# Ten weight tiles of a decoder kernel, each 96 bytes longer

## The chip, the cores and the metric

The kernel runs on one core of a Trainium2 chip. The metric is the device time of one execution in microseconds (us). Before the change the median of two runs is 1173.27 us, from 1173.14 to 1173.4.

A core has a matrix engine (TensorE, PE in the profile, with PEld for its weight loads), three engines for elementwise work (VectorE or DVE, ScalarE or ACT, GpSimd or POOL) and a sync engine (SP) that issues transfers. They work on SBUF, an on-chip memory of 128 partitions. A tile of [128, 1024] float32 takes 4096 bytes in each partition, at the same address in all of them; "address" below means this address within a partition. PSUM is the small memory that the matrix engine writes.

## What is computed

A decoder of two layers over 512 tokens of width 1024, in float32. Layer 0 mixes tokens by stick-breaking attention, layer 1 by a diagonal state-space model with a gated output. After each mixer comes a gated feed-forward block of width 2816 with a short causal convolution. All norms are scaled and shifted by vectors that one matrix-vector product makes from a conditioning vector `c`. Cut to what matters:

```
for i in range(2):
    mod = silu(c) @ w_mod[i] + b_mod[i]           # six vectors of 1024
    h = rms_norm(x) * (1 + sc1) + sh1
    y = attention(h) if i == 0 else ssm(h)         # weights w_qkv, w_o / w_in, w_glu, w_o
    x = x + g1 * y
    h = rms_norm(x) * (1 + sc2) + sh2
    up = conv3(h @ w_up[i]) + conv_b[i]            # 1024 -> 2 * 2816
    x = x + g2 * ((silu(gate(up)) * val(up)) @ w_down[i])
out = rms_norm(x) * (1 + sc) + sh
```

## The kernel before

**Products in three parts.** All large products run in the matrix engine's float32r type. To keep the precision, each operand is split into a high part and a low part, and `mm3` (L169) issues three matmuls: high by high (L171), high by low (L174), low by high (L175). In the names of the profile `up_h` is the high part of a tile of `w_up`, `up_l` its low part, and `hH`, `hL` are those of the activations. Each matmul has the weights as its stationary operand (128 x 128, loaded by a LDWEIGHTS just ahead of it) and 512 or 256 columns of activations as the moving one. In the projection to `v` alone (L592, L652) it is the other way round: the activations are loaded and the weights move.

**How a weight tile is made.** `load_w` (L147) takes a tile `raw` of [128, 1024] float32 from the pool `wp` (tag `wraw`, three buffers) and has SP load 512 KB into it (L163). ScalarE copies it into the high part `wh` (L165), and VectorE subtracts that from `raw` into the low part `wl` (L166). High parts have the tag `wH`, low parts `wL`, with `NW = 5` buffers each (L161, L162): these are the ten tiles of the change. For `w_v` the same tags are used by `high` (L570) and for `wv0` (L605). A buffer is given out again when its last matmul has read it. `load_w(own=...)` (L158) takes other tiles instead: two weights at the head of a block have a pool of their own (`head_w`, L178), whose names in the profile are `upo`, `win` and `uph` with the number 0 or 1; their neighbours 2 and 3 use the ten tiles.

**Who orders the work.** The engines have a queue each and run in order. A planner puts the instructions in order by modelled times; `pe_pin` and `keep_in_program_order` fix some of them by hand, and `follow` (L141) ties the splits of the feed-forward blocks into one line on ScalarE and one on VectorE. Semaphores make every instruction wait for its operands, and for the last reader of the memory that it writes; pools with `reuse_waits="tile"` wait for just those earlier tiles whose addresses they take.

**Where tiles lie.** Pools stack up from the low end of SBUF in the order in which they are opened: `const`, `wp` (three `wraw`, five `wH`, five `wL`), `xp` (the residual `x`), `hp` (`hH`, `hL`), `np` (buffers of the norms), and above them the pools of the current block. The pools opened with `side="right"` stack down from the high end: `gemv` (`cact`, `wg`), and at times the pool of `head_w` or that of the last norm. Tiles are rounded up to 32 bytes. In the program's map of before, taken modulo 512 bytes:

| tiles | start modulo 512 |
|---|---|
| `wraw`, all ten of `wH` and `wL` | 320 |
| `x`, `hH`, `hL`, `acc`, `nt2`, most tiles of the blocks (`ca`, `gH`, `gL`, `kz`) | 320 |
| `sq`, `nt1`, `dg` | 64 |
| right side: `cact`, `wg`, high and low parts of `head_w` | 480 |

Where the two stacks come closest, in attention, 1184 bytes are free between them.

**Stages.** Attention takes the first 250 us of the profile, feed-forward block 0 the time to about 610 us, the state-space layer that to about 780 us, and feed-forward block 1 with the last norm the rest. In block 0 GpSimd prepares tables for the state-space layer (`ssm_prep`, L984), in steps placed between the block's units; its first write there is a memset of the tile `tb` (L1103), which takes memory that a `head_w` tile had held.

Of the kernel before, what the change touches and what calls it, by code (L numbers as in the profile page):

```python
# [9 lines left out]
F32R = mybir.dt.float32r  # L10
# [7 lines left out]
P = 128  # L18
T = 512
D = 1024  # L20
# [9 lines left out]
NC = T // CH  # L30
EPS = 1e-6
NW = 5
MIDK = 1
STATK = 0
HEADK = 6
# [54 lines left out]
def _trunk(ctx, tc, I, out, tap):  # L90
# [3 lines left out]
    def pool(name, bufs=1, **kw):  # L94
        return ctx.enter_context(tc.tile_pool(name=name, bufs=bufs, **kw))

    cp = pool("const")
    wp = pool("wp")
# [48 lines left out]
    def load_w(src, n=D, name="w", own=None, lined=False):  # L147
        raw = wp.tile([P, D], F32, tag="wraw", bufs=3, name=name + "_r")
        if isinstance(own, list):

            pin["load"] = SP.dma_start(raw, src)
            cols = slice(0, D // 2), slice(D // 2, D)
            for q, cs in enumerate(cols):
                pe_pin(S.activation(own[q], raw[:, cs], AF.Copy))
            for q, cs in enumerate(cols):
                pe_pin(V.tensor_tensor(own[2 + q], raw[:, cs], own[q].bitcast(F32), ALU.subtract))
            return own[:2], own[2:]
        if own:  # L158
            wh, wl = (own.tile([P, D], F32R, tag=name + g, name=name + g) for g in ("_h", "_l"))
        else:  # L160
            wh = wp.tile([P, D], F32R, tag="wH", bufs=NW, name=name + "_h")  # L161
            wl = wp.tile([P, D], F32R, tag="wL", bufs=NW, name=name + "_l")  # L162
        pin["load"] = SP.dma_start(raw[:, :n], src)  # L163
        order = follow if lined else lambda eng, fn: fn()
        order("S", lambda: S.activation(wh[:, :n], raw[:, :n], AF.Copy))  # L165
        pin["split"] = order("V", lambda: V.tensor_tensor(wl[:, :n], raw[:, :n], wh[:, :n].bitcast(F32), ALU.subtract))  # L166
        return wh, wl
# [10 lines left out]
    def head_w(srcs, nm):  # L178
        hx = ExitStack()
        own = hx.enter_context(tc.tile_pool(name=f"hw{nm}", bufs=1, side="right", reuse_waits="tile"))  # L180
        return hx, [load_w(src, name=f"{nm}{q}", own=own if q < 2 else None) for q, src in enumerate(srcs)]
# [72 lines left out]
    def pe_pin(ins):  # L254
        tc.keep_in_program_order(ins)
# [34 lines left out]
    def rstd_bc(R, cr, pl, pinned=False):  # L290
        bc = bank(pl, "rbc")
        ins = PE.matmul(bc[:, cr], ones, R["dg"][:, cr], start=True, stop=True)
        if pinned:
            pe_pin(ins)
        R["bc"][cr.start] = bc
# [68 lines left out]
    def out_proj(wsrc, rhs, gcol, acc2, nm, tail=TAIL, perm=False, n=D, after=lambda: None, part=(), last=None, head=None, getw=None, step=lambda: None, early={}):  # L364
        nk = len(rhs)
        whole = KD - (tail if acc2 is not None else 0)

        lined = getw is not None
        getw = getw or (lambda mt: early[mt] if mt in early else load_w(wsrc(mt), n=n, name=f"{nm}{mt}"))

        def cols(ap, cr):
            return half_cols(ap, cr) if perm and cr != FULL else ap[:, cr]

        def run(ps, w, cr, mid={}, k0=0, pinned=False):
            for k in range(k0, nk):
                if k in mid:
                    mid[k]()
                mm3(cols(ps, cr), wk(w, k), (cols(rhs[k][0], cr), cols(rhs[k][1], cr)), k == 0, k == nk - 1, k in mid or pinned)
# [32 lines left out]
        for q, (mt, w, ps) in enumerate(ws):  # L411
# [3 lines left out]
            if q == 2:  # L415
                mid[MIDK if nk > 6 else MIDN] = lambda: rstd_bc(R, ca, aux, True)
            run(ps, w, cb, mid, pinned=True)
# [12 lines left out]
    def ffn(l, R, prep=None, last=None, hook=lambda: None):  # L430
# [4 lines left out]
        with ExitStack() as fc:  # L435
# [11 lines left out]
            def split_next(lined=True):  # L447
                if todo:
                    src, n, nm = todo.pop(0)
                    made.append(load_w(src, n=n, name=nm, lined=lined))  # L450
# [95 lines left out]
    def attention(acc):  # L546
        with ExitStack() as av_, ExitStack() as ac:
# [20 lines left out]
                return raw  # L568

            def high(k):  # L570
                w = [wp.tile([P, D], F32R, tag=f"w{g.upper()}", bufs=NW, name=f"wv{k}_{g}") for g in "hl"]
                pe_pin(S.activation(w[0], raws[k], AF.Copy))
                return w

# [27 lines left out]
            pe_pin(SP.dma_start(raw0, I["w_v"][0:P, :]))  # L602
            raws = {1: loads(1)}
            SP.dma_start(small[:, NMOD:], I["small"][:, NMOD:])
            wv0 = [wp.tile([P, D], F32R, tag=f"w{g.upper()}", bufs=NW, name=f"wv0_{g}") for g in "hl"]  # L605
            idle = pin["idle"]
            gv_mul(1, 0)
            idle(NIDLE[2])
# [75 lines left out]
            prod0(vo[4:], HI)  # L684
            prod0(vo[4:], LO)
            w = high(1)
            for k in range(1, KD):
                def mid():
                    nxt[0] = high(k + 1) if k < KD - 1 else None
                    pe_pin(V.tensor_tensor(w[1], raws[k], w[0].bitcast(F32), ALU.subtract))  # L690
                    if k < KD - 1:
                        gv(1, k + 1)

                nxt = [None]
                gv(0, k)
                norm_tile(h, k, rb, a, mod[:, 0:KD], FULL, True, None, mid)
                if k + 2 < KD:
                    raws[k + 2] = loads(k + 2)
                prods(k, w)
                w = nxt[0]  # L700
# [771 lines left out]
    for k in range(KD):  # L1472
# [4 lines left out]
        if k:  # L1477
            pe_pin(V.tensor_tensor(acc, acc, sq, ALU.add))
    R = attention(acc)
    for k in range(KD):  # L1480
        tap(f"x1_{k}", x[k])
# [161 lines left out]
```

## Time and profile before

| | |
|---|---|
| median of two runs | 1173.27 us (1173.14 to 1173.4) |
| the profiled execution's own time | 1172.41 us |
| its span, first to last instruction | 1170.6 us |
| PE (matmul) busy | 1156.1 us, 99% of the span |
| PEld (weight load) busy | 966.5 us, 83% |
| DVE busy | 855.1 us, 73% |
| ACT busy | 564.7 us, 48% |
| POOL busy | 274.0 us, 23% |
| granted clock of the matrix engine, mean | 0.995 |
| moved by DMA | 211.01 MB, mean 180 GB/s |

A busy matmul lasts from its start to its modelled end, and the next one starts before that end. So the busy share says that the matrix engine always had something in flight, and the distance from one start to the next says how fast it went; the two are read apart in what follows. The rows of the groups have, after the name of the operation, the tiles written and read, the shape and the count, then the busy time in us and the mean duration of one in ns, then the idle time of the engine just before, with what ended it.

### The profile page before, as it was taken

How to read it: one execution, taken by the hardware profiler on the slowest of the kernel's cores; microseconds unless marked ns; L12 is line 12 of the kernel's file. 1: busy time of each engine (PE TensorE's matmuls, PEld its weight loads, DVE VectorE, ACT ScalarE, POOL GpSimd, SP SyncE). 2: the span in 40 equal slices, each digit the busy share in tenths (PEclk: the TensorE clock that was granted, in tenths of full speed). 3: DMA queues.
4: the chain of work that ended last, by engine and by line, in shares of the span. 5: the costliest groups of instructions: out<-in, count | busy, mean ns of one | idle time of the engine just before them, and what ended most of it. 6: DMA issues, size and time to landing. Idle time of an engine off the chain costs nothing.

```text
span 1170.6 us, 16595 instructions
## 1 busy us (share of the span) xinstructions
PE 1156.1 (99%) x6242; PEld 966.5 (83%) x6242; DVE 855.1 (73%) x1311; ACT 564.7 (48%) x896; POOL 274.0 (23%) x278
## 2 busy tenths in 40 slices
PE   8999999999999999999999999999999999999997
PEld 7888787798788878888889888789888888888887
DVE  6969889675997657697767698887698278734655
ACT  6755667456452234413346587547443144422443
POOL 2001110000398799979700000000000000000013
PEclk8999999999999999999999999999999999999999
DMA  8874555322267758697756598671176356432322
GB/s 326 297 267 138 193 174 169 126 91 70 75 206 252 236 165 250 203 306 242 236 148 221 172 350 286 206 253 54 43 231 219 103 157 187 130 120 74 93 68 73
DMA packets 91618, 211.01 MB, mean 180 GB/s; under 512 B 19601, under 2 KB 37905, under 8 KB 91538
## 3 DMA queue, kind: packets, MB, share of 16 engines
q1 hardware_dynamic: 78562, 191.08, 50.6%
q0 software_dynamic: 4656, 16.78, 4.3%
q10 hardware_dynamic: 8320, 2.10, 0.8%
q8 instruction: 49, 0.80, 0.3%
q14 instruction: 31, 0.25, 0.1%
HBM read 188.68 MB, written 21.24 MB: 179 GB/s over the span
## 4 chain that ended last, share of the span: by engine, by line
PE 80%; POOL 8%; DMA 4%; DVE 4%; ACT 1%; issue 1%; SPq 0%; POOLq 0%; ACTq 0%; DVEq 0%
PE up L171 11%; PE up L174 11%; PE up L175 11%; PE dn L171 5%; PE dn L174 5%; PE dn L175 5%; PE o L831 2%; PE t L815 2%; PE wo L171 1%; PE u L174 1%; PE u L171 1%; PE wo L174 1%; PE wo L175 1%; PE u L175 1%; PE q L175 1%
## 5 line engine op out<-in xcount | busy, mean ns | idle before, releaser
L171 PE MATMUL up<-hH,up_h 128*128 128x512 f32 x640 | 249.6, 390 | 0.3 <-DVE ca L465 0.3
L175 PE MATMUL up<-hH,up_l 128*128 128x512 f32 x640 | 249.2, 389 | 0.3 <-DVE up_l L166 0.3
L174 PE MATMUL up<-hL,up_h 128*128 128x512 f32 x640 | 249.2, 389 | 0.0
L465 DVE SCALAR_TENSOR_TENSOR ca<-up,small,ca 128x511 f32<-128x511 f32 (+1 forms) x176 | 131.7, 748 | 120.9 <-ACT ca L463 117.6
L171 PE MATMUL dn<-gH,dn_h 128*128 128x512 f32 (+1 forms) x394 | 145.0, 369 | 0.0
L174 PE MATMUL dn<-gL,dn_h 128*128 128x512 f32 (+1 forms) x394 | 144.4, 367 | 0.0
L175 PE MATMUL dn<-gH,dn_l 128*128 128x512 f32 (+1 forms) x394 | 144.4, 366 | 0.0
L171 PEld LDWEIGHTS up<-hH,up_h 128*128 128x128 f32 x640 | 120.1, 188 | 26.3 <-issue 1.7
L175 PEld LDWEIGHTS up<-hH,up_l 128*128 128x128 f32 x640 | 120.2, 188 | 25.6 <-DVE up_l L166 0.8
L174 PEld LDWEIGHTS up<-hL,up_h 128*128 128x128 f32 x640 | 120.2, 188 | 24.5
L463 ACT ACTIVATE ca<-up,small 128x512 f32<-128x512 f32 x88 | 68.2, 775 | 149.3 <-PE up L175 149.3
L1515 POOL TENSOR_SCALAR xa<-x,Anorm_out 128x256 f32<-128x256 f32 x7 | 5.8, 828 | 569.1 <-DVE x L359 569.1
L202 DVE SCALAR_TENSOR_TENSOR wg<-wg,cact 128x1024 f32<-128x1024 f32 x96 | 120.7, 1276 | 13.2 <-DMA wg<-in_w_modT_dram 13.1
L165 ACT ACTIVATE up_h<-up_r 128x1024 fp32r<-128x1024 f32 x80 | 84.2, 1052 | 80.1 <-PE dn L174 58.2
L166 DVE TENSOR_TENSOR up_l<-up_r,up_h 128x1024 fp32r<-128x1024 f32 x80 | 113.3, 1417 | 9.9 <-ACT up_h L165 9.0
L359 DVE SCALAR_TENSOR_TENSOR x<-dn,mod,x 128x512 f32<-128x512 f32 (+1 forms) x55 | 37.4, 680 | 72.4 <-PE dn L175 72.4
L171 PEld LDWEIGHTS dn<-gH,dn_h 128*128 128x128 f32 x394 | 74.3, 189 | 12.8 <-issue 0.6
L174 PEld LDWEIGHTS dn<-gL,dn_h 128*128 128x128 f32 x394 | 74.3, 189 | 12.1
L175 PEld LDWEIGHTS dn<-gH,dn_l 128*128 128x128 f32 x394 | 74.3, 189 | 12.1
L165 ACT ACTIVATE dn_h<-dn_r 128x1024 fp32r<-128x1024 f32 (+1 forms) x48 | 46.6, 982 | 48.7 <-PE dn L174 40.3
L166 DVE TENSOR_TENSOR dn_l<-dn_r,dn_h 128x1024 fp32r<-128x1024 f32 (+1 forms) x48 | 60.5, 1261 | 1.6 <-ACT dn_h L165 1.3
L481 ACT ACTIVATE gH<-gm 128x512 fp32r<-128x512 f32 x44 | 27.1, 617 | 69.3 <-DVE gm L477 69.3
(349 smaller groups left out, 2317.1 us busy)
## 6 DMA issues: line engine op xcount, KB each, us to landing
up_r<-in_w_up_dram SPq DMA_DIRECT2D x80, 512.0 KB
wg<-in_w_modT_dram SPq DMA_DIRECT2D x71, 512.0 KB
dn_r<-in_w_down_dram SPq DMA_DIRECT2D x32, 512.0 KB
wg<-in_w_modT_dram POOLq DMA_DIRECT2D x25, 512.0 KB, 4.8
wgs<-in_w_modT_dram SPq DMA_DIRECT2D x16, 512.0 KB
dn_r<-in_w_down_dram SPq DMA_DIRECT2D x16, 384.0 KB
wv_r<-in_w_v_dram SPq DMA_DIRECT2D x8, 512.0 KB
wk_r<-in_w_qk_dram SPq DMA_DIRECT2D x8, 512.0 KB
```

The source lines that it names most:

```text
L165: order("S", lambda: S.activation(wh[:, :n], raw[:, :n], AF.Copy))
L166: pin["split"] = order("V", lambda: V.tensor_tensor(wl[:, :n], raw[:, :n], wh[:, :n].bitcast(F32), ALU.subtract))
L171: ins = PE.matmul(ps, ah, bh, start=start, stop=False)
L174: PE.matmul(ps, ah, bl, start=False, stop=False)
L175: PE.matmul(ps, al, bh, start=False, stop=stop)
L202: mul = lambda: V.scalar_tensor_tensor(w, w, 1.0, cact, ALU.mult, ALU.mult, accum_out=raw[:, col:col + 1])
L359: add = lambda: V.scalar_tensor_tensor(xs, pv, gate, xs, ALU.mult, ALU.add)
L463: follow("S", lambda: S.activation(ca, ps, AF.Identity, bias=small[:, cb:cb + 1], scale=tapw[2]))
L465: follow("V", lambda: V.scalar_tensor_tensor(ca[:, q:], ps[:, :T - q], tapw[2 - q], ca[:, q:], ALU.mult, ALU.add))
L481: follow("S", lambda: S.activation(gh, m, AF.Copy))
L815: pe_pin(PE.transpose(pt[:, c:c + P], wts[pr][h2][i][:, j * P:(j + 1) * P], ident))
L831: pe_pin(PE.matmul(po[pr][h2 * HD:(h2 + 1) * HD, j * P:], vn[:, j, hd:hd + HD], src, start=j == 0, stop=j == 3))
```

## The change

The five `wH` and five `wL` buffers are allocated with 1024 + 24 float32 columns, 4192 bytes, and only the first 1024 columns are used. This holds at all three places that allocate under these tags. No instruction is added or removed.

```
+WPAD = 24
...
-            wh = wp.tile([P, D], F32R, tag="wH", bufs=NW, name=name + "_h")
-            wl = wp.tile([P, D], F32R, tag="wL", bufs=NW, name=name + "_l")
+            wh = wp.tile([P, D + WPAD], F32R, tag="wH", bufs=NW, name=name + "_h")[:, :D]
+            wl = wp.tile([P, D + WPAD], F32R, tag="wL", bufs=NW, name=name + "_l")[:, :D]
...
-                w = [wp.tile([P, D], F32R, tag=f"w{g.upper()}", bufs=NW, name=f"wv{k}_{g}") for g in "hl"]
+                w = [wp.tile([P, D + WPAD], F32R, tag=f"w{g.upper()}", bufs=NW, name=f"wv{k}_{g}")[:, :D] for g in "hl"]
...
-            wv0 = [wp.tile([P, D], F32R, tag=f"w{g.upper()}", bufs=NW, name=f"wv0_{g}") for g in "hl"]
+            wv0 = [wp.tile([P, D + WPAD], F32R, tag=f"w{g.upper()}", bufs=NW, name=f"wv0_{g}")[:, :D] for g in "hl"]
```

4192 is a multiple of 32, and 96 more than eight times 512. So the ten buffers begin at 320, 416, 0, 96, 192 (high) and 288, 384, 480, 64, 160 (low) modulo 512. Every tile stacked above them moves up by 960 bytes: what began at 320 then begins at 256, what began at 64 begins at 0. The `wraw` buffers below and the right side stay where they are.

## The prediction

> **What bounds the kernel now.** I read the page first, for the engine that sets the time and for the waits beside it.
>
> ```profile
> span 1170.6 us, 16595 instructions
> PE 1156.1 (99%) x6242; PEld 966.5 (83%) x6242; DVE 855.1 (73%) x1311; ACT 564.7 (48%) x896; POOL 274.0 (23%) x278
> PE 80%; POOL 8%; DMA 4%; DVE 4%; ACT 1%; issue 1%; SPq 0%; POOLq 0%; ACTq 0%; DVEq 0%
> L171 PE MATMUL up<-hH,up_h 128*128 128x512 f32 x640 | 249.6, 390 | 0.3 <-DVE ca L465 0.3
> L175 PE MATMUL up<-hH,up_l 128*128 128x512 f32 x640 | 249.2, 389 | 0.3 <-DVE up_l L166 0.3
> L174 PE MATMUL up<-hL,up_h 128*128 128x512 f32 x640 | 249.2, 389 | 0.0
> L171 PE MATMUL dn<-gH,dn_h 128*128 128x512 f32 (+1 forms) x394 | 145.0, 369 | 0.0
> L166 DVE TENSOR_TENSOR up_l<-up_r,up_h 128x1024 fp32r<-128x1024 f32 x80 | 113.3, 1417 | 9.9 <-ACT up_h L165 9.0
> ```
>
> The matrix engine is busy for 1156.1 of 1170.6 us, and four fifths of the chain that ended last are its own. Its largest groups wait for nothing: over 1,920 matmuls of `up` it stood idle 0.6 us, and only 0.3 of that for a weight's low part. Making the ten tiles sooner is therefore worth next to nothing; the change can only tell if it alters how fast matmuls follow each other. For that I read the chain in order of time, in two short stretches of feed-forward block 1, where a piece is the distance to the next start: first 512 columns, then 512 and 256 at the block's end.
>
> ```profile
> 1049.78 0.23 PE dn L175
> 1050.01 0.23 PE dn L171
> 1050.46 0.23 PE dn L175
> 1050.69 0.23 PE dn L171
> ...
> 1142.94 0.23 PE dn L175
> 1143.40 0.12 PE dn L175
> 1143.52 0.12 PE dn L171
> 1143.64 0.12 PE dn L174
> ```
>
> From one L171 to the next are three matmuls: 1050.69 - 1050.01 = 0.68 us, 227 ns each for 512 columns. For 256 columns it is 120 ns. The difference of 107 ns over 256 columns is 0.418 ns a column, so 512 columns stream in 214 ns and 256 in 107, and either way 13 ns are left over that do not depend on the columns. These 13 ns a matmul are all that a better place for the weights could win on this engine.
>
> **The change part by part.** It removes and adds no instruction, no transfer and no wait that I can find; it changes addresses. There are four kinds of reader and writer to go through.
>
> *Weight loads and matmuls.* Some 4,600 of the 6,242 matmuls take their weights from the ten tiles: 1,920 of `up`, 1,182 of `dn` (three times 394), about 1,500 of the projections and the output products. All of them run today with weights and activations both at 320 modulo 512. The trace has one group of loads that mixes two places: the heads of the feed-forward blocks, where `upo` 0 and 1 lie at 480, which is 32 modulo 64 as half of the new places are, and `upo` 2 and 3 in the ten tiles at 320. And it has loads from 64 (`q_sq`, `q_nt`) against a moving tile at 320. These are the views of the tiles, with the shortest, middle and longest duration in ns:
>
> ```profile
> L171 PEld LDWEIGHTS up<-hH,up_h x640: 186/188/192, 269.1 to 1125.8; 128*128 128x128 f32 x160
> L171 PEld LDWEIGHTS up<-hH,upo_h x56: 187/188/193, 259.2 to 286.9; 128*128 128x128 f32 x56
> L174 PEld LDWEIGHTS up<-hL,upo_h x56: 186/188/193, 259.6 to 287.1; 128*128 128x128 f32 x56
> L798 PEld LDWEIGHTS z<-kz,q_sq x32: 187/189/192, 82.7 to 217.2; 128*128 128x128 f32 x32
> L798 PEld LDWEIGHTS z<-kz,q_nt x32: 187/188/193, 82.9 to 217.7; 128*128 128x128 f32 x32
> ```
>
> If the place mattered by more than a few ns, the mixed group would fall into two halves, and its longest would stand away from 192. It does not. The distance between starts in that head, again from the chain in order of time:
>
> ```profile
> 264.18 0.47 PE up L171 x4
> 264.65 0.12 PE up L174
> 264.77 0.12 PE up L175
> ...
> 265.48 0.12 PE up L175
> 265.60 0.47 PE up L171 x4
> ```
>
> From 264.18 to 265.60 are twelve matmuls of 256 columns, six on tiles at 480 and six on tiles at 320: 1.42 / 12 = 118 ns, against the 120 of the block's end, where all tiles lie at 320. If the place at 480 took away the 13 ns or doubled them, the mean would be 113.5 or 126.5 (half of them moved by 13). It is 118, near neither. I take 0 ns a matmul. For the bounds I use the resolution of these rows: middle values that agree within 1 ns, so 1 ns either way, and 4,600 x 1 ns = 4.6 us either way.
>
> *The splits.* ScalarE and VectorE write the ten tiles, and VectorE reads one of them beside `raw`, which stays at 320. Their durations are set by something else, as the same subtraction in two stretches shows, 500 to 600 us with GpSimd at work and 900 to 1000 us without:
>
> ```profile
> L166 DVE TENSOR_TENSOR up_l<-up_r,up_h 128x1024 fp32r<-128x1024 f32 x12 | 23.7, 1974 | 0.0
> ...
> L166 DVE TENSOR_TENSOR up_l<-up_r,up_h 128x1024 fp32r<-128x1024 f32 x16 | 19.5, 1219 | 0.5
> L165 ACT ACTIVATE up_h<-up_r 128x1024 fp32r<-128x1024 f32 x16 | 16.8, 1052 | 17.5 <-PE dn L174 17.5
> ...
> L165 ACT ACTIVATE upo_h<-upo_r x4: 1060/1062/1063, 233.3 to 241.2; 128x1024 fp32r<-128x1024 f32 x4
> L166 DVE TENSOR_TENSOR upo_l<-upo_r,upo_h x4: 1219/1226/1227, 234.4 to 242.3; 128x1024 fp32r<-128x1024 f32 x4
> ```
>
> The last two rows hold two splits into tiles at 480 and two into tiles at 320: 1060 to 1063 and 1219 to 1227 ns, nothing between the places. And a split is hidden: it runs a unit ahead of its matmuls, which waited 0.3 us in all for `up_l`. Even 8 ns more on each (1227 - 1219) stays under that cover. Without it, 8 ns on 80 + 48 splits of `up` and `dn` would be 1 us. What is late next if a split grew is the freeing of `raw` and with it the next load; by the row of `up_l` above the matrix engine would notice only after VectorE's lead is used up.
>
> *The tiles above.* `x`, `hH`, `hL` and the blocks' tiles move by 960 bytes, from 320 to 256. 960 is 15 x 64, so each keeps its place modulo 64. Moving and loaded tiles keep their distance in the products that do not use the ten tiles. I take 0, inside the same 1 ns a matmul.
>
> *Waits for memory.* The left stack comes 960 bytes nearer to the fixed right one. The closest point has 1184 bytes free, so 224 remain and everything fits. Where a new left tile takes the memory of a freed right one, or the reverse, the pairs shift: going through the map, the one pair that could matter is `tb`, which lay over the freed high part of `upo` 0 alone and will also touch its low part. GpSimd's timeline shows the cover:
>
> ```profile
> 286.14 0.13 POOL L1103 MEMSET tb<- 128x16 f32 x1 [99.42 <-PE up L174]
> 286.19 0.14 POOL L1104 MEMSET tb<- 128x16 f32 x1
> 308.13 0.23 POOL L990 TENSOR_TENSOR tt<-tb,si 128x16 f32<-128x16 f32 x1 [21.81 <-ACT si L1045]
> ```
>
> The low part's last reader follows the high part's within a few matmuls, under 2 us. Behind the memset on GpSimd stands the step at 308.13, which waits 21.81 us for ScalarE's sine anyway. The delay is hidden; without that cover it would cost GpSimd under 2 us. Another pair is a late one: `brow` of the last norm will touch memory of `gzL7`, which was freed when the state-space layer ended, over 200 us earlier. 0 for both.
>
> **The sum.** 0 (loads and matmuls) + 0 (splits) + 0 (tiles above) + 0 (waits) = 0, against the profiled execution's own 1172.41 us (a span of 1170.6 and 1.8 around it). The median of the runs shown is 1173.27, 0.9 above that execution, so I state the forecast on the median: 1173.3 us.
>
> **The rivals.**
>
> *A: the 13 ns are a clash of places.* When all weights and activations start at the same place modulo 512, the load of the next weights and the stream of the current matmul could meet in the same part of the memory, and spread places would end that. For it speaks that the 13 ns appear with 512 and with 256 columns alike, as a fixed toll for each load would. Against it: the mixed head, 118 ns with half its tiles at another place, and that a toll from a clash should vary with what else is read, while the pieces above repeat. All of it gone on 4,600 matmuls is 60 us: 1173.3 - 60 = 1113 us. If half the ten places gain, 1143.
>
> The Trainium skill, "TensorE: Matmul & The Clock Gate", section "Wait — 56ns, not 53.3ns?", puts the fixed part of a warm matmul at about 2.5 ns, where this trace has 13; by that an estimated 10.5 ns a matmul would be open to such a cause, 48 us here and 1125 us. Against that the skill's "SBUF — State Buffer", section "Who interferes with whom", gives the matrix engine two independent read ports and says that it never waits on anyone; by that there is no clash and the time stays, as the mixed head's 118 against 120 ns has it too.
>
> *B: places that are odd multiples of 32 cost a fetch (slower).* Five of the ten new places (416, 96, 288, 480, 160) are 32 modulo 64; today none of the ten is. If a load from such a place needed one more access, and the load were what makes up the 13 ns, each matmul on these five would start later. The price from the rows: the spread of the mixed group, 193 - 187 = 6 ns, on half of 4,600 matmuls: 14 us, 1187 us. It decides only from 10 ns on (2,300 x 10 = 23 us is 2%). Against it: `upo` 0 and 1 lie at such places now, and their group is no longer at the middle, 188, nor in its starts, 118.
>
> *C: the addresses do not matter, but the program is not the same.* Buffers of a tag could be given out in another order, or a wait could appear that I did not see, so that a late step of GpSimd's tables holds up block 0, where the chain runs through POOL (8%). The order comes from modelled times and names, not from addresses, so I see no way. The price by the largest single hold-up shown, 21.81 us of cover lost once: 1195 us.
>
> **How the numbers follow.** No change, 0.90: 1173.3 us, with 1168.7 to 1177.9 by the 1 ns either way. A in full or by half, 0.05. B, 0.04, of which a quarter passes 2%. C, 0.01. Left out on either side of 1168 to 1178 are A, B, C and about a tenth of the main case, so the range is 1168 to 1178. About 2% is what a measurement of this kernel can tell from no change, here 1149.8 to 1196.7. A gives faster in most of its cases, 0.04. B beyond its point, and C if more than one such hold-up came together, give slower, 0.02. Within 2% remains 0.94.
>
> **What would show it.** Right, if the groups of `up` keep 389 and 188 ns, if three matmuls in block 1 still take 0.68 us from L171 to L171 and the narrow ones 0.12, if the subtraction stays at 1219 ns in the stretch 900 to 1000 us, and if GpSimd's step at 308.13 still ends a wait for `si`. Rival A would show as 0.64 to 0.67 us for three matmuls and a matching gain in every stage, most in the feed-forward blocks. Rival B would show as two kinds of weight loads in one group, and as a pitch that alternates from unit to unit as the buffers go round. C would show as a new name in the waits of PE or POOL. I am wrong if the time leaves 1168 to 1178 while the clock stays at 0.995.

## The result and the profile after

The changed kernel takes 1191.24 us (1190.47 to 1192.0) against 1173.27: a ratio of 1.015, with a 95% interval of 1.013 to 1.017. The forecast was 1173.3 with a range of 1168 to 1178. The change makes the kernel 18 us slower, 1.5%, and the forecast of no change was wrong.

These are the lines of the page after that answer to those of before. The change adds one source line at the top, so L171 of before is L172 here, L174 is L175, L175 is L176.

```profile
span 1188.6 us, 16595 instructions
PE 1176.5 (99%) x6242; PEld 966.4 (81%) x6242; DVE 857.6 (72%) x1311; ACT 564.7 (48%) x896; POOL 271.7 (23%) x278
PE 95%; DVE 2%; ACT 1%; DMA 1%; POOL 0%; issue 0%; SPq 0%; POOLq 0%; DVEq 0%; ACTq 0%
L176 PE MATMUL up<-hH,up_l 128*128 128x512 f32 x640 | 253.1, 395 | 0.3 <-DVE up_l L167 0.3
L175 PE MATMUL up<-hL,up_h 128*128 128x512 f32 x640 | 252.8, 395 | 0.0
L172 PE MATMUL up<-hH,up_h 128*128 128x512 f32 x640 | 252.8, 395 | 0.0
L172 PEld LDWEIGHTS up<-hH,up_h 128*128 128x128 f32 x640 | 120.2, 188 | 29.6 <-issue 1.2
L167 DVE TENSOR_TENSOR up_l<-up_r,up_h 128x1024 fp32r<-128x1024 f32 x80 | 115.7, 1447 | 2.3 <-ACT up_h L166 1.4
```

The instructions are the same in number, and the matrix engine still waits for next to nothing. But it is busy for 1176.5 us instead of 1156.1, 20.4 more, and idle for 12.1 (1188.6 - 1176.5) instead of 14.5. A matmul of `up` lasts 395 ns instead of 389 or 390. The weight loads still last 188 ns. So the time was not lost in a wait: the matmuls follow each other more slowly. The chain of work that ended last, in order of time, shows by how much (block 1, matmuls of 512 columns; each line has the start and the distance to the next piece, in us):

```profile
1064.16 0.24 PE dn L172
1064.39 0.24 PE dn L175
1064.63 0.23 PE dn L176
1064.87 0.23 PE dn L172
...
1073.22 0.23 PE dn L172
```

From the L172 at 1064.16 to the one at 1073.22 there are thirteen groups of three, 39 matmuls: 9.06 / 39 = 232 ns. Before it was 227. The stretch from 900 to 1000 us, in which the matrix engine runs these wide products alone, says the same in counts: 443 matmuls before, 431 after. The figures of a line are the length of the stretch, the busy time of the matrix engine with its count of matmuls, the granted clock, the share of time in which the DMA engines were busy, and GB/s. The clock is 1.00 in both, so a lower clock is not the cause. First before, then after:

```profile
900.00:1000.00 100.00, 100.00 (x443) 1.00 0.53 150
```

```profile
900.00:1000.00 100.00, 100.00 (x431) 1.00 0.50 149
```

### The profile page after: what moved, and what is told of

It reads as the page before. It is cut to its first block, busy times and chain, and to the rows that moved or that the text cites. A ratio compares the mean times of both kernels' runs of the same rounds, so it can differ in the third digit from the quotient of the medians.

```text
span 1188.6 us, 16595 instructions
## 1 busy us (share of the span) xinstructions
PE 1176.5 (99%) x6242; PEld 966.4 (81%) x6242; DVE 857.6 (72%) x1311; ACT 564.7 (48%) x896; POOL 271.7 (23%) x278
## 4 chain that ended last, share of the span: by engine, by line
PE 95%; DVE 2%; ACT 1%; DMA 1%; POOL 0%; issue 0%; SPq 0%; POOLq 0%; DVEq 0%; ACTq 0%
PE up L172 13%; PE up L175 13%; PE up L176 13%; PE dn L172 7%; PE dn L175 7%; PE dn L176 7%; PE o L832 2%; PE t L816 1%; PE wo L172 1%; PE u L175 1%; PE wos L172 1%; PE wos L175 1%; PE wos L176 1%; PE u L172 1%; PE u L176 1%; PE wo L175 1%
## 5 line engine op out<-in xcount | busy, mean ns | idle before, releaser
L176 PE MATMUL up<-hH,up_l 128*128 128x512 f32 x640 | 253.1, 395 | 0.3 <-DVE up_l L167 0.3
L175 PE MATMUL up<-hL,up_h 128*128 128x512 f32 x640 | 252.8, 395 | 0.0
L172 PE MATMUL up<-hH,up_h 128*128 128x512 f32 x640 | 252.8, 395 | 0.0
L172 PE MATMUL dn<-gH,dn_h 128*128 128x512 f32 (+1 forms) x394 | 146.5, 373 | 0.0
L176 PE MATMUL dn<-gH,dn_l 128*128 128x512 f32 (+1 forms) x394 | 146.2, 371 | 0.0
L175 PE MATMUL dn<-gL,dn_h 128*128 128x512 f32 (+1 forms) x394 | 146.1, 371 | 0.0
L172 PEld LDWEIGHTS up<-hH,up_h 128*128 128x128 f32 x640 | 120.2, 188 | 29.6 <-issue 1.2
L176 PEld LDWEIGHTS up<-hH,up_l 128*128 128x128 f32 x640 | 120.1, 188 | 29.2 <-DVE up_l L167 0.8
L175 PEld LDWEIGHTS up<-hL,up_h 128*128 128x128 f32 x640 | 120.3, 188 | 28.3
L167 DVE TENSOR_TENSOR up_l<-up_r,up_h 128x1024 fp32r<-128x1024 f32 x80 | 115.7, 1447 | 2.3 <-ACT up_h L166 1.4
L172 PEld LDWEIGHTS dn<-gH,dn_h 128*128 128x128 f32 x394 | 74.0, 188 | 14.6 <-issue 0.6
L175 PEld LDWEIGHTS dn<-gL,dn_h 128*128 128x128 f32 x394 | 74.1, 188 | 14.1
L176 PEld LDWEIGHTS dn<-gH,dn_l 128*128 128x128 f32 x394 | 74.1, 188 | 13.9
```

The lines of the kernel that those rows point to most:

```text
L172: ins = PE.matmul(ps, ah, bh, start=start, stop=False)
L175: PE.matmul(ps, ah, bl, start=False, stop=False)
L176: PE.matmul(ps, al, bh, start=False, stop=stop)
```

## The experiments

**Three whole kernels and one of matmuls alone.** The change does two things at once. It spreads the ten weight tiles, and it moves all that lies above them, the activations among it, by 960 bytes. Theory 1 says that the distance between the places of weights and activations decides, theory 2 the spread, theory 3 the odd multiples of 32 (rival B). The ratio of each run is against executions of the kernel before in the same round, whose median was 1174.9 us for the first three runs, 1173.32 for `shift256` and `shift64`, and 1173.87 for `headmatch`.

*Run shift*: the weights as before, only the move.

```
-    x = [xp.tile([P, T], F32, tag=f"x{k}", name=f"x{k}") for k in range(KD)]
+    x = [xp.tile([P, T + (0 if k else 240)], F32, tag=f"x{k}", name=f"x{k}")[:, :T] for k in range(KD)]
```

> The ten weight tiles stay as before (all at 320 modulo 512); the first tile of x is 960 bytes longer instead, so that everything above, the activations hH and hL among it, moves to 256 as in the changed kernel. Theory 1 (match: a 512-column matmul takes 227 ns only where the weights and the moving tile begin at the same place modulo 512, some 232 to 235 elsewhere): slower, 1185 to 1195 us, and three matmuls of block 1 take about 0.70 us instead of 0.68. Theory 2 (spread: what costs is that consecutive weight loads begin at different places): no change, 1171 to 1176 us. Theory 3 (odd multiples of 32 cost a fetch, rival B): no change, 1171 to 1176 us, since 320 is a multiple of 64.

Measured: 1191.97 us, ratio 1.015 (1.0131 to 1.0169). That is the whole loss, with all ten weight tiles at 320 as before. Theories 2 and 3 fall. The profile shows the same slower matmuls as the changed kernel:

```profile
L171 PE MATMUL up<-hH,up_h 128*128 128x512 f32 x640 | 252.9, 396 | 0.0
```

*Run spread_back*: the changed kernel, with the activations back at 320.

```
 WPAD = 24
...
-    x = [xp.tile([P, T], F32, tag=f"x{k}", name=f"x{k}") for k in range(KD)]
+    x = [xp.tile([P, T + (0 if k else 16)], F32, tag=f"x{k}", name=f"x{k}")[:, :T] for k in range(KD)]
```

> The ten tiles have their 96 bytes more, as in the changed kernel, and the first tile of x is 64 bytes longer, so that all above moves by 1024 and begins at 320 again; one of the ten tiles has that same place. Theory 1 (match): nearly as slow as the changed kernel, 1186 to 1193 us. Theory 2 (spread): as slow, 1188 to 1193 us. Theory 3 (odd multiples of 32): as slow, 1188 to 1193 us. A fourth, that only the move of the activations costs: 1171 to 1176 us.

Measured: 1190.32 us, ratio 1.0134 (1.0114 to 1.0155). Moving the activations back does not help while the weights stand elsewhere. Together with the run before: each half of the change alone costs the whole or almost the whole, as it must if the distance counts.

*Run even*: all places multiples of 64.

```
-WPAD = 24
+WPAD = 16
```

> The ten tiles get 64 bytes more each instead of 96: their places are all multiples of 64 (320, 384, 448, 0, 64 and 128, 192, 256, 320, 384), and the activations begin at 448. Theory 3 (odd multiples of 32): no change, 1171 to 1177 us. Theories 1 and 2: slower, 1184 to 1195 us.

Measured: 1185.88 us, ratio 1.0093 (1.007 to 1.0117). Slower with no odd multiple of 32 among the ten places, so rival B's mechanism is out a second time. That the loss is smaller was not foreseen; the grid further down accounts for it.

*Run places*: matmuls alone, 96 of them a case; the decoder is left out. `...` stands for lines that are not shown.

```
CASES += [("w" + "abcdefghijklmno"[q], 512, 0, 0, 32 * (q + 1), 32 * (q + 1)) for q in range(15)]
...
for u in range(4):
    for k in range(8):
        hi, lo = at(2, k, P, wh, P), at(3, k, P, wl, P)
        a, b = at(0, k, T, mh, n), at(1, k, T, ml, n)
        for w, m, s in ((hi, a, 0), (hi, b, 1), (lo, a, 2)):
            tc.keep_in_program_order(nc.tensor.matmul(ps[:, :n], w, m, start=k == 0 and s == 0, stop=k == 7 and s == 2))
```

> A kernel of matmuls alone, with no other engine at work: 96 matmuls a case in the order high by high, high by low, low by high, with the place of the moving tiles and of the weights set case by case (its output is not the decoder's, it leaves all of that out). Moving tiles at 0, both weights at 0, 32, 64 and so on to 480. Theory 1: 227 ns from start to start at 0 and 230 to 236 ns at every other place, whether the weights stand at an odd multiple of 32 or not. Theory 2: 227 ns in all cases where high and low weights have one place, more only in the cases named low and lowfar. Theory 3: 227 ns at multiples of 64, more at the odd multiples of 32. With 256 columns all theories expect 118 to 120 ns, as the profiles of before and after have it.

These are the rows of the high by high matmuls in the views of the cases' tiles, from one execution. After the count come the shortest, middle and longest duration in ns, then the first and the last start in us. Between the two starts lie 31 groups of three, 93 matmuls. `same` has all at one place; `wa`, `wb`, `wc`, `wf`, `wh`, `wi`, `wn` have the weights 32, 64, 96, 192, 256, 288 and 448 bytes above the moving tiles; `four` has them 4 bytes above; `both` and `bothodd` have weights and moving tiles at 256 and at 96; `low` and `lowfar` have the low weights alone 96 and 256 bytes off, `act` the low activations alone 64 bytes off. `narrow`, `nb` and `nh` have 256 columns, with the weights 0, 64 and 256 bytes above.

```profile
L54 PE MATMUL same<-mh,wh x32: 389/389/389, 47.4 to 68.5; 128*128 128x512 f32 x32
L54 PE MATMUL wa<-mh,wh x32: 392/395/396, 69.2 to 90.9; 128*128 128x512 f32 x32
L54 PE MATMUL wb<-mh,wh x32: 393/396/398, 91.5 to 113.3; 128*128 128x512 f32 x32
L54 PEld LDWEIGHTS wb<-mh,wh x32: 188/188/188, 91.3 to 113.0; 128*128 128x128 f32 x32
L54 PE MATMUL wc<-mh,wh x32: 391/397/400, 114.0 to 135.7; 128*128 128x512 f32 x32
L54 PE MATMUL wf<-mh,wh x32: 388/388/398, 181.1 to 202.4; 128*128 128x512 f32 x32
L54 PE MATMUL wh<-mh,wh x32: 389/389/389, 225.5 to 246.6; 128*128 128x512 f32 x32
L54 PE MATMUL wi<-mh,wh x32: 392/395/396, 247.3 to 269.0; 128*128 128x512 f32 x32
L54 PE MATMUL wn<-mh,wh x32: 388/388/398, 359.3 to 380.6; 128*128 128x512 f32 x32
L54 PE MATMUL four<-mh,wh x32: 388/392/399, 403.7 to 425.3; 128*128 128x512 f32 x32
L54 PE MATMUL both<-mh,wh x32: 389/389/389, 470.5 to 491.6; 128*128 128x512 f32 x32
L54 PE MATMUL bothodd<-mh,wh x32: 387/389/397, 492.3 to 513.4; 128*128 128x512 f32 x32
L54 PE MATMUL low<-mh,wh x32: 393/397/398, 536.5 to 558.1; 128*128 128x512 f32 x32
L54 PE MATMUL lowfar<-mh,wh x32: 389/389/393, 558.8 to 579.9; 128*128 128x512 f32 x32
L54 PE MATMUL act<-mh,wh x32: 387/395/398, 580.6 to 602.1; 128*128 128x512 f32 x32
L54 PE MATMUL narrow<-mh,wh x32: 278/283/283, 602.8 to 614.0; 128*128 128x256 f32 x32
L54 PE MATMUL nb<-mh,wh x32: 281/281/283, 625.7 to 636.6; 128*128 128x256 f32 x32
L54 PE MATMUL nh<-mh,wh x32: 281/283/283, 693.9 to 705.1; 128*128 128x256 f32 x32
```

The starts are printed to 0.1 us; the trace has them in ns, and the figures here are rounded from those. `same`: 21.1 us / 93 = 227 ns. `wa` and `wb`: 233 ns. `wc`: 234 ns. `wf`: 21.3, 229 ns. `wh`: 21.1 again, 227 ns. The row of `wi` repeats that of `wa`, and that of `wn` repeats `wf`, each 256 bytes further. So the time from start to start of wide matmuls depends on the distance between weights and activations modulo 256 bytes, not 512; it is shortest at distance zero, wherever the common place is (`both`, `bothodd`), and 4 bytes of distance already cost nearly 6 ns (21.6 / 93 = 232). Theory 1 was right about the distance but not about its period: it had expected 230 to 236 ns at 256 too, and at 192. One operand out of place is nearly as bad as all (`low` 21.6 us, `act` 21.5), and 256 bytes for one alone are again free (`lowfar` 21.1).

There is a rival to the period: the program gives the cases eight places in PSUM in turn, so `wi` writes where `wa` wrote. But `both` writes where `wc` wrote, and takes 21.1 us against 21.7: it is not the place in PSUM. No other engine is at work during the cases and next to no transfer (1 GB/s), so the cause lies within the matrix engine and its reads and writes. The durations of the weight loads stay at 188 ns in the wide cases.

With 256 columns it is the other way round: 11.2 / 93 = 120 ns at distance 0 and at 256, but 118 at 64 and 117 at 96. All theories had expected 118 to 120 here.

**What the table says about the whole kernel.** Two more runs put a number on it: the same pad in `x` with 256 and with 64 bytes.

```
-    x = [xp.tile([P, T], F32, tag=f"x{k}", name=f"x{k}") for k in range(KD)]
+    x = [xp.tile([P, T + (0 if k else 64)], F32, tag=f"x{k}", name=f"x{k}")[:, :T] for k in range(KD)]
```

> Weights as before at 320 modulo 512, the first tile of x 256 bytes longer, so that the activations begin at 64. In the kernel of matmuls alone the pace depended on the distance modulo 256 only. If that holds in the whole kernel: no change, 1171 to 1177 us, and 0.68 us for three matmuls of block 1. If the place modulo 512 decides, as the change has it: 1185 to 1195 us.

Measured: 1175.04 us, ratio 1.0017 (1.0004 to 1.0029). The activations moved 256 bytes away from the weights modulo 512, and at most 0.3% is lost; 512 is not the period. The stretch from 900 to 1000 us holds 443 matmuls, as before, where the run shift holds 430. In `shift64` the 64 in the edit above is a 16.

> The same with 64 bytes: the activations begin at 384, the weights stand 64 below them where in the run named shift they stood 64 above. If the table of the matmuls alone carries over (228.9 ns at 192 modulo 256, 226.7 at 0, 233.4 at 64): 2.2 ns on some 3,960 wide matmuls is 8.7 us, less a microsecond on the narrow ones and up to four taken up by waits, so 1177 to 1182 us. If any mismatch costs alike: 1185 to 1195 us. If the place does not matter and something else in the run named shift did: 1171 to 1177 us.

Measured: 1177.98 us, ratio 1.0045 (1.0027 to 1.0063); 4.7 us by the medians, 5.3 by the ratio. The distance of 64 bytes costs less than a third of what it costs in the run shift, where it points the other way, as `wf` (192 is 64 below 256) and `wb` (64 above) have it.

*Run places2*: other widths, another order, and a search.

```
for n, nm in ((128, "a"), (192, "b"), (320, "c"), (384, "d"), (448, "e"), (512, "f")):
    CASES += [("same" + nm, n, 0, 0, 0, 0, 4, ORD), ("off" + nm, n, 0, 0, 64, 64, 4, ORD), ("offodd" + nm, n, 0, 0, 96, 96, 4, ORD)]
ALT = ("hh", "lh", "hl")
CASES += [("altsame", 512, 0, 0, 0, 0, 4, ALT), ("altoff", 512, 0, 0, 64, 64, 4, ALT)]
CASES += [("grid", 512, 0, 32 * a, 32 * b, 32 * c, 1, ORD) for a in range(8) for b in range(8) for c in range(8)]
```

> Matmuls alone again (the decoder is left out). Part one: 128, 192, 320, 384, 448 and 512 columns with the weights at the moving tiles' place, 64 above and 96 above. If a mismatch is a toll for each weight load, it costs the same 6 ns at every width but 256, where 2 ns were gained; if it is a matter of how two periodic streams fall into step, the sign and the size go with the width. Part two: the order high by high, low by high, high by low, where no weights are loaded twice in a row: 227 at the same place and about 233 at 64 above if the repeat does not matter. Part three: 512 combinations of places of the low activations, the high and the low weights, all in steps of 32 bytes, 24 matmuls each: does any place go under 226.7 ns? I expect none, since 226.7 is the lowest of the 21 wide cases so far.

The same kind of rows (`same` has all at one place, `off` the weights 64 and `offodd` 96 bytes above; the letter behind is the width: c 320, d 384, e 448 columns; `altsame` and `altoff` have the other order; ns are again from the trace's own starts):

```profile
L54 PE MATMUL samec<-mh,wh x32: 309/309/331, 112.5 to 126.1; 128*128 128x320 f32 x32
L54 PE MATMUL offc<-mh,wh x32: 307/308/310, 126.6 to 140.2; 128*128 128x320 f32 x32
L54 PE MATMUL samed<-mh,wh x32: 334/334/337, 154.7 to 170.8; 128*128 128x384 f32 x32
L54 PE MATMUL offd<-mh,wh x32: 338/338/338, 171.4 to 187.8; 128*128 128x384 f32 x32
L54 PE MATMUL samee<-mh,wh x32: 362/365/374, 205.0 to 223.8; 128*128 128x448 f32 x32
L54 PE MATMUL offodde<-mh,wh x32: 362/362/363, 243.9 to 262.5; 128*128 128x448 f32 x32
L54 PE MATMUL altsame<-mh,wh x32: 389/389/389, 329.7 to 350.8; 128*128 128x512 f32 x32
L54 PE MATMUL altoff<-mh,wh x32: 393/396/398, 351.5 to 373.2; 128*128 128x512 f32 x32
L54 PE MATMUL grid<-mh,wh x4096: 387/394/409, 373.9 to 3224.1; 128*128 128x512 f32 x196
```

At 320 columns the distance of 64 makes no difference (13.6 us both); at 384 the common place is the faster one, 16.1 against 16.4 us, 173 against 177 ns; at 448 the distance of 96 is faster than none, 18.6 against 18.8 us, 200 against 203 ns. The other cases show that width and distance act together: at 384 columns a distance of 96 costs nothing (173 ns), at 448 one of 64 gains under 1 ns, and at 128 and 192 columns every case takes 111 or 112 ns. So it is no toll for each load: sign and size go with the width, which speaks for two periodic streams falling into step or not. The order of the three matmuls does not matter (21.1 and 21.7 us, as `same` and `wb`).

Over the whole grid the mean from start to start is (3224.1 - 373.9) / (4095 x 3) = 232 ns. Each of its 512 combinations has 24 matmuls only, the first of them still beside those of the case before. From the fourth to the last, the one with all places equal comes to 227.3 ns, and one other to 227.7 (low activations at 64, high weights at 192, low weights at 64); none is faster. So the kernel before already stood at the best place that was found.

The grid also holds the pairs of the whole kernels. The j-th high and the j-th low tile are used together, so a kernel has five pairs of distances; the run even has, for instance, 128 and 192, 192 and 0, 0 and 64, 64 and 128, 128 and 192 bytes above the activations. The mean of the five combinations of the grid, counted from the fourth to the last start, stands here beside the mean distance that follows a 512-wide matmul of `mm3` in the kernel's own trace (some 3,930 distances, those under 300 ns):

| kernel | grid, ns | its own trace, ns |
|---|---|---|
| before, shift256 | 227.3 | 227.4 |
| shift64 | 228.8 | 229.3 |
| even | 231.8 | 231.6 |
| spread_back | 232.3 | 232.4 |
| after | 233.1 | 232.9 |
| shift | 233.4 | 233.1 |

The order comes out, and each value within 0.5 ns, from addresses alone. It also says why the run even loses less: its pair 192 and 0 takes 229.0 ns, and only the two pairs 128 and 192 take as much as the run shift.

**The heads of before.** The prediction had leaned on the heads of the feed-forward blocks. This run puts their own tiles where the activations are.

```
-    cact = gvp.tile([P, D], F32, tag="cact", name="cact")
+    cact = gvp.tile([P, D + 40], F32, tag="cact", name="cact")[:, :D]
```

> The kernel before with its right-hand tiles moved down by 160 bytes (cact is 160 bytes longer), so that the heads' own weight tiles begin at 320 modulo 512 like the activations, instead of 480. Match theory: the wide matmuls at the end of each head, which stood 232 ns apart where the tiles mixed, come to 227 or little above, and the narrow ones go from 118 or 119 ns to 120. Some 60 wide matmuls times 5 ns is 0.3 us less, some 250 narrow ones times 1 ns is 0.3 us more: no change that can be measured, 1171 to 1176 us. If the 232 ns of the heads come from their order (another tile for every matmul) and not from the places: the wide ones stay at 232.

Measured: 1175.2 us, ratio 1.0003 (0.9987 to 1.0018), no change, as expected. The chain in order of time, at the end of the head where the matmuls are 512 wide, first before, then in this run:

```profile
283.29 0.23 PE up L174
283.52 0.24 PE up L175
...
286.08 0.25 PE up L175
```

```profile
281.04 0.23 PE up L174
281.27 0.23 PE up L175
...
285.13 0.23 PE up L174
```

Before, twelve matmuls took 286.08 - 283.29 = 2.79 us, 232 ns each; now eighteen take 285.13 - 281.04 = 4.09, 227 ns each. It was the places and not the order. The narrow ones go the other way, as expected:

```profile
263.54 0.48 PE up L171 x4
264.02 0.12 PE up L174
...
264.98 0.48 PE up L171 x4
```

Twelve of them now take 264.98 - 263.54 = 1.44 us, 120 ns each, where the prediction had read 118.

## Why the prediction was wrong

**The step that failed** is the first, "Weight loads and matmuls", where I took 0 ns a matmul with 1 ns either way. It should have been 5.5 for the wide ones: by the table above they went from 227.4 to 232.9 ns, so some 4,000 of them lose 4,000 x 5.5 = 22 us. Added up over the two traces, the distances that follow them grow by 22.3 us, those that follow `mm3`'s 256-wide matmuls shrink by 0.5, the long ones of 300 ns and more shrink by 3.7, and all others keep their sum. That leaves 18.1 us, the loss. In the page's terms, the matrix engine's busy time rose by 20.4, its idle time fell by 2.4, and 20.4 - 2.4 = 18.0 is the loss in the span.

Three readings led there. The first was to take the weight loads' durations as a gauge: for 512 columns they are 188 ns at every place, while the pace changes beside them. Of the two groups of loads that were to show another place, the one from 64 (`q_sq`, `q_nt`) was no witness at all: it stands 256 bytes from its moving tile at 320, where `wh` loses nothing. The second was the choice of stretch. The head that mixes two places was the right place to look, but I took its matmuls of 256 columns, where a distance costs nothing or gains 2 to 3 ns, and carried the 118 against 120 over to 512 columns. The third was the test itself: I asked only whether the 13 ns were gone or doubled, and passed over the 2 ns between 118 and 120, which are more than the 1 ns either way that I allowed. Some 4,000 of the 6,242 matmuls are 512 wide (1,920 of them `up`'s), and the same head ends in such wide ones; their 232 ns stood in the trace of before, as the rows above show, and spoke against the forecast.

**The tiles above.** I wrote that products which do not use the ten tiles keep their distance, and booked 0 for the move. That does not hold for the heads, whose own tiles stay on the right side while the activations move. Above all, nearly all products do use the ten tiles, and for them the move alone, as the run shift shows, costs all of it.

**The splits** were right. The subtraction takes 1220 ns in the stretch 900 to 1000 us, against 1219, and by the row of L176 at the start the matmuls wait 0.3 us for it in all:

```profile
L167 DVE TENSOR_TENSOR up_l<-up_r,up_h 128x1024 fp32r<-128x1024 f32 x13 | 15.9, 1220 | 0.4
```

**The waits for memory** were right as well. GpSimd's memset of `tb` now waits for the low part's last reader (L176), and the step behind it still waits for ScalarE:

```profile
288.49 0.13 POOL L1104 MEMSET tb<- 128x16 f32 x1 [99.93 <-PE up L176]
...
310.23 0.23 POOL L991 TENSOR_TENSOR tt<-tb,si 128x16 f32<-128x16 f32 x1 [21.57 <-ACT si L1046]
```

**Rival A** had the right suspicion, that the places of weights and activations bear on each other, with the sign reversed: the common place is the best one, and spreading is the harm. The 13 ns a matmul beside the columns, 227 ns against 214, stay at the best place with nothing else running. By the Trainium skill, "TensorE: Matmul & The Clock Gate", section "Wait — 56ns, not 53.3ns?", some 2.5 ns would be left; these streams of load and matmul do not bear that out. By the Trainium skill, "SBUF — State Buffer", section "Who interferes with whom", the engine's two read ports are independent and it never waits on anyone. By that the distance would not matter; in the run of matmuls alone it is worth up to 7 ns a matmul (227 to 234). Whether the reads at these ports are where the time goes is not shown.

**Rival B** came near in time, 1187 us, by luck and for a wrong reason: the run even is slow without an odd multiple of 32, and `bothodd`, all at 96, is as fast as `same`. **Rival C** did not occur.

That the distance between the two operands' places sets the pace is shown. What stays open is what in the engine has the period of 256 bytes. That the width changes the sign points to a phase between two streams; no run here shows the mechanism itself.

## What to carry to other kernels

An allocation that only shifts addresses need not be free on a kernel bound by matmuls: check the distance between the stationary and the moving operand's start, modulo 256 bytes, and for float32r matmuls of 512 columns with a weight load each keep it at zero. Other widths were measured at a few distances only, and other types not at all. When arguing from a mixed stretch that something does not matter, take the rows of the same shape as the work that sets the time, and the distance from start to start rather than the duration of a load. Where a pad moves a tile, list what it pushes along.

## What was not expected of the hardware

- The pace of 512-column float32r matmuls, each with its own weight load, runs from 227 ns with both operands' starts equal modulo 256 bytes to 233 ns at 64 bytes of distance and 234 at 96, with no other engine at work; 4 bytes give 232.
- The sign goes with the width: 120 ns at distance zero against 118 at 64 bytes with 256 columns, 173 against 177 with 384, no difference with 320; with 448 columns 203 against 200 at 96 bytes.
- The direction counts: with weights 64 bytes above the activations a matmul takes 233 ns, with 64 below 229.
